# One decoder layer in float32 pairs: four weight buffers that begin at 0, 32, 64 and 96 modulo 128

## The chip, the cores and the metric

The kernel runs on one core of one Trainium2 chip. The metric is the device time of one execution in microseconds, as the median of several runs; lower is better. A core has a matrix engine (TensorE, PE in the profile, with its weight loads shown apart as PEld), a vector engine (VectorE, DVE), a scalar engine (ScalarE, ACT), GpSimd (POOL) and SyncE (SP), which here only issues DMAs. They work on one on-chip memory of 128 partitions, SBUF. The results of PE go to a second one, PSUM. An address below is a byte offset within a partition, the same in all 128.

## What is computed

One layer of a decoder trunk on 256 rows of 2048 numbers, all in float32: a feed-forward block, a mixing block (differential attention beside a matrix memory), a second feed-forward block, and a last normalization. Nearly all the work is in the products with the weights:

```python
x = x + 0.5 * swiglu(rmsnorm(x, ffn1_norm[l]), ffn1_w_gate[l], ffn1_w_up[l], ffn1_w_down[l])
h = rmsnorm(x, mix_norm[l])
a_q, a_k, a_v, m_q, m_k, m_v, m_o, m_i, m_f = jnp.split(h @ w_in[l], split_idx, axis=-1)
...
x = x + jnp.concatenate([y_a, y_b], axis=-1) @ w_out[l]
x = x + 0.5 * swiglu(rmsnorm(x, ffn2_norm[l]), ffn2_w_gate[l], ffn2_w_up[l], ffn2_w_down[l])
return rmsnorm(x, final_norm)
```

with `swiglu(h, g, u, d) = (silu(h @ g) * (h @ u)) @ d`, 2048 columns in, 5632 inside.

## The kernel before

**Split products.** PE multiplies in a faster form of float32 (`float32r`, F32R in the code) that keeps fewer bits. To keep the accuracy, each operand is split in two: `hi` is the operand rounded to F32R, `lo` is what is left. A product is then made of three matmuls into the same place of PSUM: x's hi by the weights' hi (line 182), x's lo by the weights' hi (line 183) and x's hi by the weights' lo (line 185). These three lines are in `mms`, which gets a list of jobs, issues lines 182 and 183 for each of them, and then line 185 for each. In all three x is the operand that is loaded into PE (128 rows by 128 columns, PEld), and the weights are the one that moves through it (128 rows by 512 columns in most stages).

**Where the splits come from.** Weights come by DMA into float32 tiles (`raw`, `rawp`, `late`) of the pools `wr` and `wrp`. `split` (lines 131 to 134) makes the two halves: ACT copies into the hi tile with a cast (line 133), DVE subtracts and writes the lo tile (line 134). Where a helper calls them, these two lines stand for all splits, of weights and of x; the tiles' names tell them apart (`wh<-raw`, `xs<-xsum`).

**The tiles that the change touches.** `pair_tiles` (line 162) takes a hi and a lo tile, `wh` and `wl`, from the pool `wsp`. It is called by `split_w`, `tile_by_tile`, `split_two` and `bare`, always with two rows of weights, 512, 392, 384 or 256 columns wide; 2 x 512 x 4 bytes are 4096, the size of every buffer. The pool has four buffers for each of the two names and gives them out in turn, so a unit of work uses one `wh` buffer and the `wl` buffer of the same number, the next unit the next ones. A unit is two jobs (6 matmuls) or four (12 matmuls), mostly. Before the change all eight buffers begin at a multiple of 128 bytes, and so do x's tiles `xs` and `xt` (pool `slots`, 4096 bytes each) and the float32 tiles of the weights.

**One stage is narrower.** The first pair of the mixing projection is 392 columns wide for one weight matrix and 384 for the other. In a tile of two rows by 392 columns the second row begins 1568 bytes behind the first.

**Work tiles.** The pool `work` has eight buffers under one name. Most are 512 float32 wide, 2048 bytes; the largest that share the name hold 2 x 257. Among them are `xsum`, `hg`, `xg`, `sg`, `ds`, `us` and `mv`.

**Order.** The program is one stream per engine. Splits are issued at a raised priority, up to 400 places ahead of the matmuls that use them, but not further than the four buffers allow: ACT's copy into a `wh` buffer waits until line 183 has read it for the last time, DVE's into `wl` until line 185 has.

Of the kernel before, what the change touches and what calls it, by code (L numbers as in the profile page):

```python
# [10 lines left out]
F32R = mybir.dt.float32r  # L11
# [6 lines left out]
P = 128  # L18
# [6 lines left out]
CW = 512  # L25
# [35 lines left out]
def tile_trunk_layer(ctx: ExitStack, tc: tile.TileContext, x, xt, par, bias_if, lamv, fnorm,  # L61
# [16 lines left out]
    def nm(s):  # L78
        uid[0] += 1
        return f"{s}_{uid[0]}"  # L80
# [79 lines left out]


    def pair_tiles(pool, tag, shape):
        return (pool.tile(shape, F32R, tag=tag + "h", name=nm(tag + "h")),
                pool.tile(shape, F32R, tag=tag + "l", name=nm(tag + "l")))

    def split_w(raw, pieces):
        hi, lo = pair_tiles(wsp, "w", list(raw.shape))
        with tc.high_priority(offset=AHEAD):
            o = 0
            for n in pieces:  # L170
                made = split_weights(raw[:, o:o + n, :], hi[:, o:o + n, :], lo[:, o:o + n, :])
                o += n
        splits.append(made)
        return hi, lo
# [56 lines left out]
    def tile_by_tile(w, ahead):  # L231
        raw = wr.tile([P, 3, w.shape[3]], F32, tag="raw", name=nm("raw"))
        hi, lo = pair_tiles(wsp, "w", [P, UK, w.shape[3]])
        with tc.high_priority(offset=AHEAD):
            for t in range(UK):
                ahead(0, t)
                in_turn(nc.sync.dma_start(raw[:, t, :], w[0][:, t, :]))
                made = split_weights(raw[:, t, :], hi[:, t, :], lo[:, t, :])
        splits.append(made)
        ahead(1)  # L240
        return hi, lo
# [180 lines left out]
    class Paired:  # L422
# [28 lines left out]
        def split_two(self, srcs):  # L451
            with tc.high_priority(offset=AHEAD):
                t = pair_tiles(wsp, "w", [P, 2, self.n])
                if len(srcs) == 1 and len(srcs[0].shape) == 3:
                    made = split_weights(srcs[0], *t)
                else:
                    for i, src in enumerate(srcs):
                        made = split_weights(src, t[0][:, i, :], t[1][:, i, :])
                splits.append(made)
            return t  # L460
# [807 lines left out]
```

## Time and profile before

| | us |
|---|---|
| median of 3 runs | 1763.91 |
| lowest and highest | 1763.17 and 1764.56 |
| the profiled execution, its time | 1764.66 |
| the profiled execution, its span from the first to the last instruction | 1763.0 |

The profile is one execution. A group's line gives the source line, the engine, the operation, the tiles written and read, the shape, how often it ran, its busy time and the mean duration of one in ns, and then how long the engine had been idle just before, and what ended that. Matmuls overlap in the records: one starts while the one before it still drains, so the mean duration of a matmul is longer than its share of PE's time. The distance from one start to the next is read from the timeline, whose rows begin with the start in us from the start of the span. In the timeline equal instructions that follow each other are merged in one row (x4), and in the windows' rows the numbers in brackets count instructions; the number behind POOL's is PE's granted clock as a share of the full one.

### The profile page before, as it was taken

To read this page: it belongs to the slowest core of one execution; us is meant where nothing else is said; L and a number is where in the kernel's file an instruction comes from. 1 tells how busy PE (TensorE), PEld (TensorE's weight loads), DVE (VectorE), ACT (ScalarE), POOL (GpSimd) and SP (SyncE) were. 2 spreads that over 40 slices of the span, in tenths; PEclk is the share of its full clock that TensorE was granted. 3 is DMA by queue.
4 is the path that set the end of the run, shared out by engine and by line. 5 is a ranking of instruction groups with operands and counts; after the bars stand their busy time and mean duration, and the time that the engine had idled before them with its cause. 6 is when DMAs were issued, how large, how long until landed. Compare 5 with 4: busy or idle time off the path is not lost.

```text
span 1763.0 us, 24479 instructions
## 1 busy us (share of the span) xinstructions
PE 1746.9 (99%) x7926; PEld 1438.9 (82%) x7926; DVE 1616.8 (92%) x2189; ACT 1266.4 (72%) x1949; POOL 428.2 (24%) x630
## 2 busy tenths in 40 slices
PE   9999999999999999999999999999999999999998
PEld 7788888888888887987888888888888877888886
DVE  7999999999999999897889999999999999999997
ACT  8666776777677768677687777776776677677765
POOL 0122332322233312022231101122332332223310
PEclk9999999999999999999999999999999999999999
DMA  9787997998799976577885667997998898799973
GB/s 365 251 253 208 259 270 251 268 292 261 214 262 266 260 234 192 186 232 220 239 239 193 205 197 216 266 268 230 248 273 264 244 261 271 238 248 270 269 254 114
DMA packets 155266, 429.72 MB, mean 244 GB/s; under 512 B 17633, under 2 KB 18945, under 8 KB 154881
## 3 DMA queue, kind: packets, MB, share of 16 engines
q0 software_dynamic: 76304, 196.66, 43.9%
q1 hardware_dynamic: 77680, 229.40, 37.8%
q10 hardware_dynamic: 1152, 2.09, 0.3%
q8 instruction: 62, 1.02, 0.2%
q14 instruction: 68, 0.55, 0.1%
HBM read 349.56 MB, written 2.10 MB: 199 GB/s over the span
## 4 chain that ended last, share of the span: by engine, by line
PE 97%; DVE 1%; ACT 1%; issue 1%; DMA 0%; SPq 0%; POOLq 0%; POOL 0%; ACTq 0%; DVEq 0%
PE acc L182 19%; PE acc L185 19%; PE acc L183 19%; PE accn L182 12%; PE accn L183 12%; PE accn L185 12%; PE tr L373 1%; DVE wl L134 0%; PE sc L1060 0%; DMA rawp<-in_wg_dram 0%; PE tr L314 0%; PE num L1011 0%; ACT wh L133 0%; PE tr L1099 0%; PE tr L802 0%
## 5 line engine op out<-in xcount | busy, mean ns | idle before, releaser
L133 ACT CAST wh<-raw 128x512 fp32r<-128x512 f32 (+2 forms) x885 | 599.7, 707 | 209.1 <-PE acc L183 69.5
L134 DVE TENSOR_TENSOR wl<-raw,wh 128x512 fp32r<-128x512 f32 (+2 forms) x885 | 674.0, 790 | 56.2 <-ACT wh L133 51.2
L133 ACT CAST wh<-rawp 128x1024 fp32r<-128x1024 f32 (+3 forms) x308 | 317.8, 1034 | 115.1 <-PE acc L183 57.8
L134 DVE TENSOR_TENSOR wl<-rawp,wh 128x1024 fp32r<-128x1024 f32 (+3 forms) x308 | 366.5, 1194 | 33.2 <-ACT wh L133 31.0
L182 PE MATMUL acc<-wh,xs 128*128 128x512 f32 (+2 forms) x956 | 370.2, 388 | 1.0 <-ACT us L503 1.0
L183 PE MATMUL acc<-wh,xs 128*128 128x512 f32 (+2 forms) x956 | 369.2, 387 | 0.0
L185 PE MATMUL acc<-wl,xs 128*128 128x512 f32 (+2 forms) x956 | 318.0, 388 | 0.8 <-DVE wl L134 0.8
L533 POOL DMA_DIRECT2D raw<-late x176 | 152.5, 1061 | 443.0 <-DVE wl L134 411.9
L182 PE MATMUL acc<-wh,xt 128*128 128x512 f32 (+2 forms) x564 | 218.4, 388 | 0.7 <-ACT wh L133 0.7
L183 PE MATMUL acc<-wh,xt 128*128 128x512 f32 (+2 forms) x564 | 217.3, 386 | 0.0
L182 PE MATMUL accn<-wh,xt 128*128 128x512 f32 (+1 forms) x552 | 215.6, 391 | 0.0
L183 PE MATMUL accn<-wh,xt 128*128 128x512 f32 (+1 forms) x552 | 214.8, 389 | 0.0
L479 DVE TENSOR_TENSOR raw<-raw 128x1024 f32<-128x1024 f32 x176 | 210.8, 1215 | 0.8
L185 PEld LDWEIGHTS acc<-wl,xs 128*128 128x128 f32 x956 | 178.6, 188 | 39.1 <-DVE wl L134 3.5
L182 PEld LDWEIGHTS acc<-wh,xs 128*128 128x128 f32 x956 | 179.8, 188 | 37.6 <-ACT us L503 1.4
L183 PEld LDWEIGHTS acc<-wh,xs 128*128 128x128 f32 x956 | 179.9, 188 | 35.6
L182 PE MATMUL accn<-wh,xs 128*128 128x512 f32 (+1 forms) x408 | 163.1, 401 | 2.3 <-ACT wh L133 2.3
L183 PE MATMUL accn<-wh,xs 128*128 128x512 f32 (+1 forms) x408 | 158.3, 389 | 0.0
L185 PE MATMUL acc<-wl,xt 128*128 128x512 f32 (+2 forms) x564 | 157.4, 386 | 0.0
L495 POOL DMA_DIRECT2D raw<-raw x92 | 78.7, 895 | 318.6 <-DVE wl L134 234.9
L185 PE MATMUL accn<-wl,xt 128*128 128x512 f32 (+1 forms) x552 | 155.1, 389 | 0.0
L185 PE MATMUL accn<-wl,xs 128*128 128x512 f32 (+1 forms) x408 | 141.4, 389 | 1.5 <-DVE wl L134 1.5
(229 smaller groups left out, 2123.7 us busy)
## 6 DMA issues: line engine op xcount, KB each, us to landing
rawp<-in_wd_dram SPq DMA_DIRECT2D x88, 512.0 KB, 5.1
raw<-late POOLq DMA_DIRECT2D x174, 256.0 KB, 5.1
raw<-in_wu_dram POOLq DMA_DIRECT2D x80, 512.0 KB, 8.1
rawp<-in_wu_dram SPq DMA_DIRECT2D x73, 512.0 KB, 5.3
rawp<-in_wg_dram SPq DMA_DIRECT2D x69, 512.0 KB, 5.0
raw<-raw POOLq DMA_DIRECT2D x92, 256.0 KB, 3.9
raw<-in_wd_dram POOLq DMA_DIRECT2D x44, 512.0 KB, 8.2
late<-in_wg_dram SPq DMA_DIRECT2D x41, 512.0 KB, 8.7
```

What stands on the lines that cost most here:

```text
L133: return (nc.scalar.copy(hi, src), nc.vector.tensor_tensor(out=lo, in0=src, in1=hi.bitcast(F32), op=ALU.subtract))
L134: nc.vector.tensor_tensor(out=lo, in0=src, in1=hi.bitcast(F32), op=ALU.subtract))
L182: nc.tensor.matmul(acc, lh, rh, start=first, stop=False, skip_group_check=on)
L183: nc.tensor.matmul(acc, ll, rh, start=False, stop=False, skip_group_check=on)
L185: newest[:] = [nc.tensor.matmul(acc, lh, rl, start=False, stop=last, skip_group_check=on)]
L373: nc.tensor.transpose(tr[:, i, hb * P:(hb + 1) * P], hs[hb][:, k * P:(k + 1) * P], ident)
L479: nc.vector.tensor_tensor(out=raw[:, 0:2, :], in0=raw[:, 0:3:2, :], in1=raw[:, 1:2, :].to_broadcast([P, 2, n]), op=ALU.add)
L495: nc.gpsimd.dma_start(raw[:, 0, :], raw[:, 2, :], accum_op=ALU.add)
L533: nc.gpsimd.dma_start(self.raws[j][:, 0, :], lates[-1][1][:, i, :], accum_op=ALU.add)
```

## The change

Each tile of `wh` and `wl` is taken as a flat row of 2 x 512 + 8 numbers, 4128 bytes in place of 4096, and the part that is used is viewed as the two rows that it was before. 4128 is 32 more than a multiple of 128, so the four buffers of a name begin at 0, 32, 64 and 96 modulo 128. The eight buffers take 256 bytes more in all, and the pools behind them move by that.

```diff
     def pair_tiles(pool, tag, shape):
-        return (pool.tile(shape, F32R, tag=tag + "h", name=nm(tag + "h")),
-                pool.tile(shape, F32R, tag=tag + "l", name=nm(tag + "l")))
+        def one(t):
+            n = math.prod(shape[1:])
+            flat = pool.tile([P, 2 * CW + 8], F32R, tag=tag + t, name=nm(tag + t))[:, 0:n]
+            return flat.rearrange("p (a b) -> p a b", a=shape[1])
+        return one("h"), one("l")
```

No instruction is added, removed or moved by it, and no tile has another shape for the instructions that use it.

## The prediction

> **What bounds the kernel now.** I read the page from the top: the engines' shares, the granted clock, the chain that ended last.
>
> ```profile
> span 1763.0 us, 24479 instructions
> PE 1746.9 (99%) x7926; PEld 1438.9 (82%) x7926; DVE 1616.8 (92%) x2189; ACT 1266.4 (72%) x1949; POOL 428.2 (24%) x630
> ...
> PE 97%; DVE 1%; ACT 1%; issue 1%; DMA 0%; SPq 0%; POOLq 0%; POOL 0%; ACTq 0%; DVEq 0%
> ```
>
> PE is busy for 99% of the span, and 97% of the chain is PE's own matmuls. So nearly nothing is waited for, and the span is the number of matmuls times the distance from one to the next. The view of waits, PE's alone, says how much room there is:
>
> ```profile
> PE accn L182 <- ACT wh L133: 2.3, 4, 0.8
> PE accn L185 <- DVE wl L134: 1.5, 2, 1.4
> PE accn L101 <- DVE touch L90: 1.3, 1, 1.3
> PE acc L182 <- ACT us L503: 1.0, 1, 1.0
> PE acc L185 <- DVE wl L134: 0.8, 1, 0.8
> PE acc L182 <- ACT wh L133: 0.7, 1, 0.7
> ```
>
> These add up to 7.6 us in 1763. If matmuls get longer, at most these few us give way; if they get shorter, the next engine in line is DVE with 1616.8 us.
>
> How many matmuls read a tile of split weights? The costliest groups, on the page:
>
> ```profile
> L182 PE MATMUL acc<-wh,xs 128*128 128x512 f32 (+2 forms) x956 | 370.2, 388 | 1.0 <-ACT us L503 1.0
> ...
> L182 PE MATMUL acc<-wh,xt 128*128 128x512 f32 (+2 forms) x564 | 218.4, 388 | 0.7 <-ACT wh L133 0.7
> ...
> L182 PE MATMUL accn<-wh,xt 128*128 128x512 f32 (+1 forms) x552 | 215.6, 391 | 0.0
> ...
> L182 PE MATMUL accn<-wh,xs 128*128 128x512 f32 (+1 forms) x408 | 163.1, 401 | 2.3 <-ACT wh L133 2.3
> ```
>
> L182 runs 956 + 564 + 552 + 408 = 2480 times. L183 and L185 stand beside it in the same loop, so 7440 of PE's 7926 matmuls stream a wh or wl tile. In all of them the weights are the moving operand (512 columns of 4 bytes in most) and x is the loaded one.
>
> The mean of 388 ns is a duration from start to end, and these overlap; what counts is the distance between starts. The timeline of PE gives it for three widths, at undisturbed places:
>
> ```profile
> 354.83 0.39 PE L183 MATMUL acc<-wh,xs 128*128 128x512 f32 x1
> 355.06 0.62 PE L185 MATMUL acc<-wl,xs 128*128 128x512 f32 x2
> 355.51 0.39 PE L182 MATMUL acc<-wh,xt 128*128 128x512 f32 x1
> ...
> 357.32 0.84 PE L185 MATMUL acc<-wl,xt 128*128 128x512 f32 x3
> ...
> 713.26 0.34 PE L182 MATMUL accn<-wh,xt 128*128 128x392 f32 x1
> ...
> 715.40 0.34 PE L182 MATMUL accn<-wh,xt 128*128 128x392 f32 x1
> ...
> 717.56 0.34 PE L182 MATMUL accn<-wh,xt 128*128 128x392 f32 x1
> ...
> 721.79 0.33 PE L182 MATMUL acc<-wh,xs 128*128 128x384 f32 x1
> ...
> 723.87 0.33 PE L182 MATMUL acc<-wh,xs 128*128 128x384 f32 x1
> ```
>
> - 512 columns: 354.83 to 357.32 holds 11 matmuls, so 226.4 ns each.
> - 384 columns: 721.79 to 723.87 is one unit of 12 (8 for wh, 4 for wl): 173.3 ns each.
> - A column therefore costs (226.4 - 173.3) / 128 = 0.415 ns, and a matmul carries a fixed 226.4 - 512 x 0.415 = 13.9 ns beside its columns.
> - 392 columns should then take 173.3 + 8 x 0.415 = 176.6 ns. Two units of 12 run from 713.26 to 717.56: 179.2 ns, 2.6 more.
>
> The stage of 392 columns is the one place where tiles already begin off 128: the second half of a unit starts 392 x 4 = 1568 bytes in, 32 past a multiple of 128. Eight further columns cost 5.9 ns there, nearly what 16 would (6.6).
>
> One more row tells whether PE's own cycles or the delivery of its operand make the distance. Here the clock was halved:
>
> ```profile
> 703.50:704.70 1.20, 1.20 (x5) 1.20 (x4) 1.20 (x3) 0.72 (x2) 0.00 (x0) 0.50 0.01 3
> ```
>
> ```profile
> 703.75 0.53 PE L182 MATMUL accn<-wh,xs 128*128 128x392 f32 x1
> 704.07 0.53 PE L183 MATMUL accn<-wh,xs 128*128 128x392 f32 x1
> 704.40 0.52 PE L182 MATMUL accn<-wh,xs 128*128 128x392 f32 x1
> 704.73 0.37 PE L183 MATMUL accn<-wh,xs 128*128 128x392 f32 x1
> ```
>
> At a granted clock of 0.50 three matmuls take 704.73 - 703.75 = 0.98 us, 327 ns each: 392 x 0.83, and nothing beside the columns. The fixed 13.9 ns and the odd 2.6 ns are gone. I read this as: at full clock the matmul waits for its moving operand to come out of SBUF, and at half clock it doesn't. Then an awkward start address costs time, and it costs it on the chain.
>
> **The change part by part.** The number of instructions, their shapes and their order stay; 32 bytes are added to each of 8 buffers, 256 = 2 x 128 in all, so the pools behind keep their place modulo 128. What moves is where wh and wl begin. A unit takes one buffer of wh and the same one of wl, in turn, so a quarter of the matmuls each has its moving operand at 0, 32, 64 and 96. Both halves of a 512-column unit share it (2048 bytes apart).
>
> *ACT and DVE*, which write these tiles, I cost at nothing. The work tiles already lie at all four places (2080 bytes apart: the largest of them has 2 x 257 x 4 bytes), while raw, wh and xs lie at 0:
>
> ```profile
> L134 DVE TENSOR_TENSOR wl<-raw,wh 128x512 fp32r<-128x512 f32 x698 | 454.4, 684 | 46.4 <-ACT wh L133 41.5 <-PE acc L185 2.7 <-DMA raw<-in_win_dram 0.8
> ...
> L134 DVE TENSOR_TENSOR xs<-xsum,xs 128x512 fp32r<-128x512 f32 x40 | 27.3, 683 | 1.5 <-ACT xs L133 1.4
> ...
> L134 DVE TENSOR_TENSOR xs<-hg,xs 128x512 fp32r<-128x512 f32 x22 | 14.5, 683 | 0.0
> ```
>
> Reading xsum or hg off 128 takes 683 ns, reading raw at 0 takes 684. If DVE did slow by 1%, that is 16 us of an engine with 146 us to spare.
>
> *Weight loads* read x, which stays; they take 188 ns, under the 226.4 of the matmul beside them:
>
> ```profile
> L182 PEld LDWEIGHTS acc<-wh,xt 128*128 128x128 f32 x564 | 105.9, 188 | 22.0 <-ACT wh L133 1.1
> ```
>
> *Loads by DMA* go to raw, rawp and late, which keep their offsets; they follow PE's pace.
>
> *The moving operand* is the whole price, and no row shows 512 columns at 32, 64 or 96. From below: minus 13.9 ns a matmul, if the fixed part came from x and weights both beginning at 0. From above: 16 columns' worth, 16 x 0.415 = 6.64 ns, at each of the three new offsets; the next step, 32 columns' worth (13.3 ns), is shut out, since 392 columns would then take 173.3 + 13.3 = 186.6 ns and take 179.2. Between the ends I go by the 392 row, the nearest: it behaves as if the operand came in pieces of 16 columns (64 bytes), 24.5 pieces counting as 25 three quarters of the way. A 512-column row that starts 32 bytes into a piece touches 33 instead of 32; one that starts at 64 touches 32. So 6.64 ns at offsets 32 and 96, nothing at 0 and 64:
>
> 7440 / 2 x 6.64 ns = 24.7 us.
>
> The price may be three quarters of that, as in the 392 row (18.5 us), and of the 7.6 us of waits some 1 us will be absorbed. What is late next is nothing new: PE stays the bound, DVE's share falls to 90%.
>
> [...]
>
> In all: the profiled execution has a span of 1763.0 and a time of 1764.66, 0.75 above the median of the three runs, 1763.91. 1763.91 + 24.7 - 1 gives **1788 us** as the median to come (span about 1787).
>
> **The rivals.**
> *No change* (1763.9): the 392 columns are rounded up by their number and not by where they lie, or the pool rounds 4128 bytes up so that the offsets don't appear at all. For it: in the 392 stage both halves would need 25 pieces wherever they start, so that row can't tell number from place; and 257-column products, whose second operand lies 1028 bytes into a work tile, go by undisturbed: six in 1.46 us with the last one 0.38 long, 216 ns apart whatever the offset.
>
> ```profile
> 858.90 1.46 PE L1011 MATMUL num<-mv,dec 128*128 128x257 f32 x6
> ...
> L1011 PE MATMUL num<-mv,dec 128*128 128x257 f32 x24 | 5.8, 379 | 0.0
> ```
>
> Against it: those are plain f32, at 216 ns for 257 columns half the speed per column, so delivery need not bind them.
>
> *Slower still* (about 1816): each change of offset also breaks the rhythm. After a short wait the timeline shows matmuls that need some time to fall back into step:
>
> ```profile
> 256.46 0.41 PE L182 MATMUL accn<-wh,xt 128*128 128x512 f32 x1
> 256.71 0.39 PE L183 MATMUL accn<-wh,xt 128*128 128x512 f32 x1
> ...
> 258.33 1.04 PE L373 MATMUL tr<-ident,sg 128*128 128x128 f32 x8
> ```
>
> From 256.71 to 258.33 are 7 matmuls, 1.62 us against 7 x 0.2264 = 1.585: some 30 ns lost. Units have 6 or 12 matmuls; at 8 on average there are 930, and 30 ns each is 28 us more, 1788 + 28. Against it: in the 392 stage the offset changes every one or two matmuls, and the loss is 2.6 ns a matmul, not 5.
>
> *Faster* (1686 at the full price): the fixed 13.9 ns is a collision in SBUF, the load of the next x (at 0) against the stream of weights (at 0), and an offset of 32, 64 or 96 keeps them apart. It decides where the fixed part depends on the distance between the two. Three quarters of 7440 at 13.9 ns are 77.6 us; the time would be 1763.9 - 77.6, less if DVE then shows. For it: the 13.9 ns is the same at 512 and 384 columns and vanishes at half clock, as a matter of SBUF would. Against it: in the 392 stage half of the matmuls already stream from 32 while x lies at 0, and the group is longer, not shorter, than its columns.
>
> [...]
>
> **How the numbers follow.** Forecast (1775 to 1795): 0.47. No change: 0.26. Slower still, through rhythm or all three offsets at 6.64 ns (37 us, 1801): 0.13. Faster: 0.14. The range has to take in the forecast and no change (0.73) and the nearer half of slower still, so 1761 to 1806. By the same cases, with 0.2% (3.5 us) as what a measurement of this kernel can tell from none: slower 0.60, same 0.26, faster 0.14.
>
> **What would show it.** Right: the granted clock is as before; the timeline of PE shows units of 512 columns at 226.4 ns in turn with units at 230 to 233, the mean duration of the L182 groups rises from 388 by about 3, the DVE rows keep 684, and PE's waits shrink. All units at 226.4: no change. One odd unit in four: all three offsets cost. A distance below 220 in any unit: the collision was real. It is wrong altogether if the time moves and the distance between matmuls in undisturbed places doesn't, through waits of PE on wh or wl.

## The result, and the profile after

The changed kernel takes 1795.64 us (median of 4 runs, 1795.45 to 1797.14), the kernel before 1764.19 in the same runs: 31.5 us more, a ratio of 1.0181 with a 95% interval of 1.0163 to 1.0199. It is slower, as forecast, by a third more than the 24 us forecast: within the stated range of 1761 to 1806, and just above the 1775 to 1795 that was given to the forecast itself. Two executions reported further down ran at a lower granted clock, the profiled one of the move by 480 bytes (2183.03 us at 0.753) and one of the kernel before (2507.51 us at 0.653), and are in none of the ratios. The page of the changed kernel, with its engines' shares, the chain and the groups that stood in the prediction (three lines were added above `mms`, so line 182 is now 185, 183 is 186 and 185 is 188):

```profile
span 1795.4 us, 24479 instructions
...
PE 1782.1 (99%) x7926; PEld 1442.7 (80%) x7926; DVE 1624.1 (90%) x2189; ACT 1270.6 (71%) x1949; POOL 429.3 (24%) x630
...
PE 98%; ACT 1%; DVE 0%; issue 0%; DMA 0%; POOLq 0%; POOL 0%; SPq 0%; DVEq 0%; ACTq 0%
...
L185 PE MATMUL acc<-wh,xs 128*128 128x512 f32 (+2 forms) x956 | 374.9, 393 | 0.9 <-ACT us L506 0.9
...
L185 PE MATMUL acc<-wh,xt 128*128 128x512 f32 (+2 forms) x564 | 220.8, 392 | 0.7 <-ACT wh L133 0.7
L186 PE MATMUL acc<-wh,xt 128*128 128x512 f32 (+2 forms) x564 | 219.6, 390 | 0.0
L185 PE MATMUL accn<-wh,xt 128*128 128x512 f32 (+1 forms) x552 | 217.3, 394 | 0.0
...
L185 PE MATMUL accn<-wh,xs 128*128 128x512 f32 (+1 forms) x408 | 165.5, 407 | 0.7 <-ACT wh L133 0.6
```

The counts are the same, PE is as busy as before (99%), and its busy time has grown by 35 us. So the loss is inside the matmuls: the groups of line 182 rose from 388, 388, 391 and 401 ns to 393, 392, 394 and 407. PE's own waits, in the view of waits of the changed kernel, shrank from 7.6 to 4.7 us:

```profile
PE accn L101 <- DVE touch L90: 1.3, 1, 1.3
PE accn L188 <- DVE wl L134: 1.2, 1, 1.2
PE acc L185 <- ACT us L506: 0.9, 1, 0.9
PE acc L185 <- ACT wh L133: 0.7, 1, 0.7
PE accn L185 <- ACT wh L133: 0.6, 1, 0.6
```

DVE, which writes the moved tiles, shows next to nothing in its groups (684 ns before):

```profile
L134 DVE TENSOR_TENSOR wl<-raw,wh 128x512 fp32r<-128x512 f32 x698 | 455.5, 686 | 53.7 <-ACT wh L133 43.6 <-PE acc L188 7.6 <-issue 0.5
```

The timeline of PE, where a row begins with the start in us, tells how far apart the matmuls start now. Between these two rows lie three whole units of 6:

```profile
354.81 0.39 PE L185 MATMUL accn<-wh,xs 128*128 128x512 f32 x1
...
359.01 0.39 PE L185 MATMUL accn<-wh,xt 128*128 128x512 f32 x1
```

18 matmuls in 4.20 us are 233.3 ns each, where 226.4 was read before. That all three units are slow, and not every second one, is the first sign that the forecast's reason was not the right one.

**Two things that the description lacks.** The addresses of the built program show that "modulo 128" hides half of what moves. The four hi buffers begin at 0, 32, 64 and 96 modulo 256. They take 4 x 4128 = 16512 bytes, which is 64 x 256 + 128, so the lo buffers behind them begin at 128, 160, 192 and 224 modulo 256. And a unit doesn't always use hi and lo buffers of the same number: the hi buffer at 0 mostly goes with the lo buffer at 192, the one at 64 with that at 128. Neither was in the prediction; the first turned out to matter.

### The profile page after: what moved, and what is told of

Read it like the earlier page. It is cut to its first block, busy times and chain, and to the rows that moved or that the text cites. A ratio compares the mean times of both kernels' runs of the same rounds, so it can differ in the third digit from the quotient of the medians.

```text
span 1795.4 us, 24479 instructions
## 1 busy us (share of the span) xinstructions
PE 1782.1 (99%) x7926; PEld 1442.7 (80%) x7926; DVE 1624.1 (90%) x2189; ACT 1270.6 (71%) x1949; POOL 429.3 (24%) x630
## 4 chain that ended last, share of the span: by engine, by line
PE 98%; ACT 1%; DVE 0%; issue 0%; DMA 0%; POOLq 0%; POOL 0%; SPq 0%; DVEq 0%; ACTq 0%
PE acc L185 19%; PE acc L188 19%; PE acc L186 19%; PE accn L185 12%; PE accn L186 12%; PE accn L188 12%; PE tr L376 1%; PE sc L1063 0%; PE tr L317 0%; PE num L1014 0%; DVE wl L134 0%; PE tr L1102 0%; DMA raw<-in_wg_dram 0%; PE tr L805 0%; ACT wh L133 0%
## 5 line engine op out<-in xcount | busy, mean ns | idle before, releaser
L185 PE MATMUL acc<-wh,xs 128*128 128x512 f32 (+2 forms) x956 | 374.9, 393 | 0.9 <-ACT us L506 0.9
L186 PE MATMUL acc<-wh,xs 128*128 128x512 f32 (+2 forms) x956 | 373.8, 392 | 0.0
L188 PE MATMUL acc<-wl,xs 128*128 128x512 f32 (+2 forms) x956 | 323.1, 393 | 0.0
L185 PE MATMUL acc<-wh,xt 128*128 128x512 f32 (+2 forms) x564 | 220.8, 392 | 0.7 <-ACT wh L133 0.7
L186 PE MATMUL acc<-wh,xt 128*128 128x512 f32 (+2 forms) x564 | 219.6, 390 | 0.0
L185 PE MATMUL accn<-wh,xs 128*128 128x512 f32 (+1 forms) x408 | 165.5, 407 | 0.7 <-ACT wh L133 0.6
L186 PE MATMUL accn<-wh,xs 128*128 128x512 f32 (+1 forms) x408 | 160.9, 396 | 0.0
```

The source lines that it names most:

```text
L185: nc.tensor.matmul(acc, lh, rh, start=first, stop=False, skip_group_check=on)
L186: nc.tensor.matmul(acc, ll, rh, start=False, stop=False, skip_group_check=on)
L188: newest[:] = [nc.tensor.matmul(acc, lh, rl, start=False, stop=last, skip_group_check=on)]
```

## The experiments

Three theories were set against each other. *Pieces* (the forecast): a row of 512 columns that begins at 32 or 96 touches one more piece of 16 columns. *Changes*: only a change of offset from unit to unit costs. *Distance*: what counts is where the moving operand (weights) lies relative to the loaded one (x), modulo some length. Each kernel is the kernel before with the edit shown, or the changed one where the diff says so.

Where all weights move, an unused tile is put ahead of the eight weight buffers, and in most of these kernels another behind them, so that the pools behind keep their place modulo 128.

**All weights at 32.**

```diff
+    wsp.tile([P, 8], F32, tag="front", name="front", bufs=1)
...
+    wsp.tile([P, 24], F32, tag="rear", name="rear", bufs=1)
```

> All eight buffers begin at 32 modulo 128 (one piece of 32 bytes ahead of them, 96 bytes behind them), x's tiles stay at 0. Piece theory (a row of 512 columns that starts at 32 touches one piece of 16 columns more, 6.64 ns): every matmul goes from 226.7 to 233.3 ns, 7440 x 6.64 ns = +49 us, 1813 us. Change theory (only a change of offset from unit to unit costs, since matmuls fall out of step): no change, 1764 us. Distance theory (what counts is where the weights lie relative to x, which is loaded at the same time): slower than before by about as much as the changed kernel or more, with no unit at 226.7 ns.

Measured: 1802.35 us against 1764.16, +38.2 (ratio 1.0218, 1.0203 to 1.0233). The timeline of this kernel's PE:

```profile
355.96 0.39 PE L183 MATMUL accn<-wh,xs 128*128 128x512 f32 x1
...
360.16 0.39 PE L183 MATMUL accn<-wh,xt 128*128 128x512 f32 x1
```

Again 18 matmuls in 4.20 us, 233.3 ns. Nothing changes from unit to unit here, so changes alone are out as the cause. Pieces and distance both stand.

**All weights at 64** (16 numbers ahead and 16 behind).

> The same with all eight buffers at 64 modulo 128, x at 0. Piece theory with 64-byte pieces: no change, 1764 us. Change theory: no change, 1764 us. Distance theory: slower, about 1790 us, as the matmuls at 64 in the changed kernel are no faster than those at 0.

Measured: 1776.39 us, +12.2 (1.0067, 1.005 to 1.0084). The timeline of PE:

```profile
355.32 0.39 PE L183 MATMUL accn<-wh,xt 128*128 128x512 f32 x1
...
360.81 0.39 PE L183 MATMUL acc<-wh,xs 128*128 128x512 f32 x1
```

24 matmuls in 5.49 us, 229 ns. Slower, which pieces of 64 bytes can't give, but by a third of what 32 costs; the 1790 of the distance theory was too high.

**Alternate 0 and 64** (the changed kernel with 64 bytes more in a buffer, not 32).

```diff
-            flat = pool.tile([P, 2 * CW + 8], F32R, tag=tag + t, name=nm(tag + t))[:, 0:n]
+            flat = pool.tile([P, 2 * CW + 16], F32R, tag=tag + t, name=nm(tag + t))[:, 0:n]
```

> Each buffer 64 bytes longer, so the four begin at 0, 64, 0 and 64, x at 0. Piece theory: no change, 1764 us. Change theory: most of the loss, since the offset changes with nearly every unit: 1785 to 1795 us. Distance theory: half of what all64 loses.

Measured: 1788.26 us, +24.1 (1.014, 1.0125 to 1.0155). This is within what the change theory gave, but it isn't shown to be the price of changes: modulo 256 these buffers lie at 0, 64, 128 and 192, hi and lo alike, and the mean of the four even kernels with these distances (0, +12.2, +35.2 and +40.4, the last two below) is already 22.0. For the question of changes the run decides nothing.

**x and weights both at 32.** The piece ahead goes into x's pool, so x's tiles and the weights move together.

```diff
+    slots.tile([P, 8], F32, tag="front", name="front", bufs=1)
...
+    wsp.tile([P, 24], F32, tag="rear", name="rear", bufs=1)
```

> x's tiles and all eight weight buffers begin at 32 modulo 128, so their distance is 0 as before the change. Piece theory: 1813 us, as with the weights alone at 32. Change theory and distance theory: no change, 1764 us.

Measured: 1764.53 us, +0.4 (1.0004, 0.9995 to 1.0013). The timeline of PE shows a unit of 6 in 1.36 us, 226.7 ns each:

```profile
354.25 0.39 PE L183 MATMUL acc<-wh,xs 128*128 128x512 f32 x1
...
355.61 0.39 PE L183 MATMUL acc<-wh,xt 128*128 128x512 f32 x1
```

Weights at 32 cost 38 us with x at 0, and nothing with x at 32. That ends the piece theory, and with it any theory in which the weights' own address counts by itself. The float32 tiles of the weights and the work tiles lie at the same place in both.

**All weights at 96, and x at 32 instead.** The first is the edit of all weights at 32, with 24 numbers ahead and 8 behind. For the second, shown here, x moves by 32 and the weights by 128.

```diff
+    slots.tile([P, 8], F32, tag="front", name="front", bufs=1)
+    wsp.tile([P, 24], F32, tag="front2", name="front2", bufs=1)
```

> All eight weight buffers at 96 modulo 128, x at 0. Piece theory is out already (x and weights both at 32 cost nothing). Distance theory: a price of its own for a distance of 96; if forward and backward count alike (96 is 32 the other way round), about that of all32, 1802 us; if only the distance ahead counts, something else between 1764 and 1802 us.

> The other way round: x's tiles at 32, all eight weight buffers at 0, so the weights lie 96 ahead of x modulo 128. Distance theory: the time of all96, whatever that is. If it was only the weights' own offset that counts, with x at 0 or 32 without effect, this gives 1764 us.

Measured: 1803.39 us with the weights at 96, 1803.27 with x at 32, against 1762.71: +40.7 and +40.6 (1.0229 both; 1.0212 to 1.0246 and 1.0214 to 1.0245). Two kernels that share only the distance, 96, share the time. The timeline of PE of the second (x at 32) has the 18 matmuls in 4.20 us too:

```profile
356.31 0.39 PE L184 MATMUL accn<-wh,xs 128*128 128x512 f32 x1
...
360.51 0.39 PE L184 MATMUL accn<-wh,xt 128*128 128x512 f32 x1
```

**Moved by 128 and by 256.** The edit of all weights at 32, with 32 numbers ahead, and with 64, and none behind. By the move of 128 the pools behind the weights move by 128 too, as they do with x and weights both at 32, where that cost nothing (+0.4 us).

> All eight weight buffers moved by 128 bytes, x at 0. If distance counts modulo 128: 1764 us, as before. If the memory's pattern is wider than 128 bytes: another time, faster or slower.

> All eight weight buffers moved by 256 bytes, x at 0. The move by 128 bytes cost 35 us, so distance does not count modulo 128. If it counts modulo 256: 1763 us, as before. If modulo 512 (x's columns are loaded in runs of 512 bytes, one at each multiple of 512, so no wider period can show): another time, at or near the 1798 us of the move by 128.

Measured: 1797.92 us by 128, against 1762.71, +35.2 (1.0199, 1.0183 to 1.0214); 1763.58 by 256, against 1763.29 (1.0002, 0.9993 to 1.0011). The timeline of PE of the move by 128:

```profile
355.14 0.39 PE L183 MATMUL accn<-wh,xs 128*128 128x512 f32 x1
...
359.33 0.39 PE L183 MATMUL accn<-wh,xt 128*128 128x512 f32 x1
```

18 matmuls in 4.19 us, 232.8 ns. And of the move by 256, with the unit of 6 back at 1.36 us:

```profile
354.49 0.39 PE L183 MATMUL acc<-wh,xs 128*128 128x512 f32 x1
...
355.85 0.39 PE L183 MATMUL acc<-wh,xt 128*128 128x512 f32 x1
```

So distance counts modulo 256, as far as one move by 256 shows. "x's tiles stay at 0, the weights at a multiple of 128" was no safe place; it was one only because the kernel before has them at a multiple of 256.

**Moved by 480 and by 192** (32 and 64 behind x modulo 256; 120 numbers ahead and 8 behind, 48 ahead and 16 behind).

> All eight weight buffers moved by 480 bytes, so they lie 32 behind x modulo 512 and 96 ahead modulo 128. If the sign makes no difference: that of all32, 1801 us. If the loss comes from weights that lie ahead of x: at or below 1763 us.

> All eight weight buffers moved by 192 bytes, x at 0; with a period of 256 that is 64 behind x. In the changed kernel a quarter of the lo matmuls lies there. If the loss depends on the size of the distance alone: that of all64, 1775 us. If ahead and behind differ: another time, up to that of all96 and all480, 1803 us.

Measured: 1802.69 us by 480, against 1763.29, +39.4 (1.0223, 1.0206 to 1.024); 1803.12 by 192, against 1762.72, +40.4 (1.0225, 1.0207 to 1.0243). Behind x, 64 costs three times what it costs ahead of it. The size of the distance alone doesn't give the price.

**Hi at 0, lo at 64.** A piece of 64 bytes between the hi and the lo buffers, another behind them.

```diff
-        return (pool.tile(shape, F32R, tag=tag + "h", name=nm(tag + "h")),
-                pool.tile(shape, F32R, tag=tag + "l", name=nm(tag + "l")))
+        hi = pool.tile(shape, F32R, tag=tag + "h", name=nm(tag + "h"))
+        if not splits:
+            pool.tile([P, 16], F32, tag="mid", name=nm("mid"), bufs=1)
+        return hi, pool.tile(shape, F32R, tag=tag + "l", name=nm(tag + "l"))
...
+    wsp.tile([P, 16], F32, tag="rear", name="rear", bufs=1)
```

> The four hi buffers of the weights at 0, the four lo buffers at 64, x at 0: the offset changes twice in every unit (4 matmuls at 0, 2 at 64, or 8 and 4). Distance alone, with a third of the matmuls at 64: a third of the 12 us of all64, 1768 us. Distance and changes (a change costs some 30 ns while the matmuls fall back into step): 1785 to 1797 us, at or above the alternate offsets of alt64, 1788.

Measured: 1786.87 us, +24.2 (1.0135, 1.012 to 1.0151). A third of the matmuls at +12.2 would give 4.1. The other 20 us are put down to the changes, twice in every unit, and the trace bears that out. The timeline of PE shows one unit:

```profile
358.14 0.39 PE L184 MATMUL accn<-wh,xt 128*128 128x512 f32 x1
...
359.05 0.63 PE L187 MATMUL accn<-wl,xt 128*128 128x512 f32 x2
359.52 0.39 PE L184 MATMUL acc<-wh,xs 128*128 128x512 f32 x1
```

Four hi matmuls in 0.91 us, 227.5 ns; two lo matmuls in 0.47 us, 235 ns, though 64 is worth 229 when nothing changes. Over the whole trace the hi matmuls start 229.4 ns apart and the lo ones 233.5. The hi matmuls come back into step slowly: the first behind a change takes 230.7 ns to the next start, the second 229.6, the third 229.2, and the sixth, in the longer units, 227.9, where the kernel before has 227.3.

**The changed kernel with its lo buffers at 0, 32, 64 and 96 too** (384 bytes between hi and lo).

```diff
-        return one("h"), one("l")
+        hi = one("h")
+        if not splits:
+            pool.tile([P, 96], F32, tag="mid", name=nm("mid"), bufs=1)
+        return hi, one("l")
```

> The changed kernel with 384 bytes between its hi and lo buffers, so that the lo buffers too begin at 0, 32, 64 and 96 modulo 512 (in the changed kernel they begin at 128, 160, 192 and 224 modulo 512). Distance alone, as the mean of the four even kernels (0, +38, +12 and +41 us): +23 us, 1786 us. Distance and changes of offset: the units at 0 and 64 cannot fall into their fast rhythm, so most matmuls go at 231 to 233 ns: 1790 to 1796 us.

Measured: 1792.73 us, +29.4 (1.0168, 1.0153 to 1.0184). The mean of the even kernels is 22.8; 6.6 us are left for changes.

All distances side by side. The last two columns are the mean distance between the starts of two 512-column matmuls that follow each other, from the traces (starts up to 260 ns apart, which leaves waits and transposes out), sorted by the addresses of the built program; for the move by 480 and for 160 there is no such number of an even kernel.

| weights ahead of x, modulo 256 | even kernel, us over before | ns apart, even kernel | ns apart, changed kernel |
|---|---|---|---|
| 0 | 0 | 227.3 | 231.3 |
| 32 | +38.2 | 233.3 | 233.1 |
| 64 | +12.2 | 229.2 | 230.8 |
| 96 | +40.7 | 233.4 | 233.5 |
| 128 | +35.2 | 232.7 | 232.8 |
| 160 | not tried | | 234.2 |
| 192 | +40.4 | 233.3 | 232.6 |
| 224 | +39.4 | | 232.0 |

These are 512 columns. In the narrower stages, whose second rows begin 1536 and 1024 bytes in, multiples of 256, the same kernels show other prices. At 384 columns the matmuls start 173.4 ns apart at a distance of 0, of 32 and of 64, 173.3 at 192, and 176.6 and 176.0 at 96 and 128 (71 matmuls in each kernel). At 256 columns 0 isn't even the best: 119.4 ns there, 116.8 at 32 and 115.6 at 192 (85 in each, starts up to 150 ns apart). The timeline of the kernel with all weights at 32 shows one unit of 12 at 384 columns:

```profile
741.31 0.34 PE L183 MATMUL acc<-wh,xs 128*128 128x384 f32 x1
...
743.39 0.34 PE L183 MATMUL acc<-wh,xt 128*128 128x384 f32 x1
```

2.08 us, the same as the unit in the prediction had at a distance of 0. So the prices at 512 columns did not hold at 384 and at 256.

## Why the prediction was right in its range, and wrong in its reason

*The bound.* PE's matmuls, the time from one start to the next, and no other engine: right. DVE and ACT cost nothing (684 and 686 ns for `wl` of 512 columns, 621 ns in both kernels for `wh`), the clock (0.998) and the counts were as before, and the waits gave way by 2.9 us where 1 was forecast.

*The price per matmul.* The step that failed is "as if the operand came in pieces of 16 columns", with 6.64 ns at 32 and 96 and nothing at 0 and 64. Weights at 32 with x at 32 cost nothing, so no piece is touched more or less. What counts in these runs is the distance of the two operands modulo 256: +38.2 us with the weights alone at 32, +40.6 with x alone at 32, +0.4 with both, +0.3 with the weights moved by 256. That the price per matmul was close is luck: at a distance of 32 or 96 the runs show 233.3 and 233.4 ns, and 226.7 + 6.64 is the same. But 64 costs too (+12.2 us), and half of the distances in the changed kernel (those of the lo buffers, a third of the matmuls) were not in the sum at all. The rival with "all three offsets at 6.64 ns" was nearer: 32 and 96 cost about that, and 64 a third of it.

*The sum by distance, made again.* Hi, two thirds of the matmuls: the mean of 0, 38.2, 12.2 and 40.7 is 22.8. Lo, one third: 35.2, 40.4, 39.4 and, untried, 160, which I put at 38 as the mean of these; 38.3. Two thirds of 22.8 and a third of 38.3 are 28.0 of the 31.5 us. The rest, some 3.5, is put down to the change of distance between units: in the last column only the units at 0 and at 64 are clearly slower than in an even kernel, by 4.0 and 1.6 ns, which over their 1239 and 1266 matmuls is 7 us. The two figures agree no better than that: the interval of the ratio alone lets the 31.5 us lie between 28.8 and 35.1. This part is worked out from the table, not tried by itself in the changed kernel.

*No change* was wrong. The buffers do begin where the change puts them, and where x is loaded from, relative to the weights, decides by up to 6.1 ns (227.3 to 233.4) how far apart matmuls of 512 columns start.

*Slower still.* That matmuls fall out of step when the offset changes is real: in the kernel with hi at 0 and lo at 64 the first behind a change takes 230.7 ns and the sixth 227.9, and 20 us are put down to it. But 28 us were put on it for the changed kernel, where a few us are left for it. The units at 32 and 96 have nothing to lose by a change: 233.1 and 233.5 ns in the changed kernel, 233.3 and 233.4 in the even ones.

*Faster.* This rival had the right pair of operands, x's load and the weights' stream, and the wrong sign: for the whole kernel a distance of 0 is the best of the seven tried, not the worst (the other six take 12.2 to 40.7 us more). The fixed 13.9 ns stays there.

*The 392 columns.* The prediction took its price from this row, and said itself that it couldn't tell number from place. The runs don't show that it was place. The second row of such a tile begins 1568 = 6 x 256 + 32 bytes in, so half of the matmuls stream from a distance of 32. But in the kernel before these start 180.4 ns apart and the other half, at 0, 178.3; both are above the 176.6 that the columns give. With all weights at 32 the two halves lie at 32 and 64, and the mean is 178.9, where it was 179.3. And 384 columns cost nothing more at 32 than at 0 (173.4 ns at both). What makes the odd 2.6 ns stays open; it was no measure of what 512 columns would pay.

*The half clock.* That the fixed part vanishes there holds in the kernel with all weights at 32 too. Its windows' row and its timeline at the lowered clock:

```profile
719.50:722.20 2.70, 2.70 (x10) 2.70 (x10) 2.70 (x5) 2.00 (x4) 0.73 (x1) 0.50 0.12 12
```

```profile
720.84 0.53 PE L183 MATMUL accn<-wh,xs 128*128 128x392 f32 x1
...
721.82 0.53 PE L184 MATMUL accn<-wh,xs 128*128 128x392 f32 x1
```

Three matmuls in 0.98 us, 327 ns, as before, where 392 columns at 0.83 ns make 325. This can't show what a distance costs at half clock, since at 392 columns this one cost nothing at full clock either (178.9 ns, and 179.3 before). The execution at a clock of 0.753, with the weights moved by 480, says more: its 512-column matmuls start 285.3 ns apart on the mean, and 512 columns at 0.415 ns make 282.2 at that clock. Of the fixed 13.9 ns, and of what this distance costs at full clock (39.4 us over 7440 matmuls, 5.3 ns each), some 3 ns are left together. That fits the prediction's reading, that the matmul waits for something at full clock only; that it waits for its moving operand to come out of SBUF is not shown.

*Open:* what repeats after 256 bytes, why 64 ahead is cheap and 64 behind is not, why 384 and 256 columns pay other prices than 512, whether distance alone counts when x lies elsewhere than at 0 or 32, and whether distances that are no multiples of 32 do better than 0. No kernel here beat the one before.

## What to carry to other kernels

When PE is the bound and streams float32r, look at the addresses of both operands of a matmul, not at one. Here, for 512 columns, it was best to keep them the same modulo 256 for all buffers of a pool: six other distances cost 12.2 to 40.7 us. A pool moved by 256 bytes cost 0.3 us, one moved by 128 cost 35.2. Don't carry a price from one width to another: the row of 392 columns, 2.6 ns above its columns, said nothing reliable about 512. One kernel that moves both operands together tells address from distance. A forecast whose number comes true isn't shown to be right in its reason: here the same 6.6 ns came from another cause, and only the kernels that moved both operands, or moved x alone, told them apart.

## What the hardware showed that was not expected

- The distance between the operands in SBUF, modulo 256 bytes, is worth up to 41 us of 1763: on the mean 227 ns from start to start of 512 columns at 0, 229 at 64, 233 at 32, 96, 128 and 192. A common offset of 32 is worth nothing (+0.4 us).
- It depends on the number of columns: at 384, distances of 32, 64 and 192 cost nothing (173.3 to 173.4 ns, as at 0), and 96 and 128 some 3 ns (176.6 and 176.0).
- The price isn't symmetric: 64 ahead +12.2 us, 64 behind +40.4 us.
- Matmuls of 512 columns at distance 0 keep to one rhythm, and lose it for some matmuls after a change of distance: with hi at 0 and lo at 64 the first after a change takes 230.7 ns and the sixth 227.9; in the changed kernel those at 0 start 231.3 ns apart, in the kernel before 227.3.
